# An encoder trunk in split float32: gates, even queries and keys projected by token and turned by DMA

## The chip, the core and the metric

The kernel runs on one core of a Trainium2 chip. A core has five engines with their own instruction streams: TensorE (PE in the profile; PEld is its weight load), VectorE (DVE), ScalarE (ACT), GpSimd (POOL) and SyncE (SP), which here only issues DMAs. The metric is the device time of one execution in microseconds. A run of the profiler gives one execution with a record of each instruction; its span, from the first to the last instruction, is a little shorter than its device time.

## What is computed

A trunk of two pre-RMSNorm residual layers and a final RMSNorm over x of 256 tokens by 2048 features, all float32. The even layer has one input projection for two head groups of eight heads each (head size 128): A is dilated sliding-window attention with an ALiBi penalty, B is 2-D neighbourhood attention with a learned position bias per head. The odd layer has C, windowed grouped-query attention with a sink logit and ALiBi (eight query heads, two key/value heads), and D, dense grouped-query attention with RMS-normalised q and k and axial rotary. Each branch has a gate as wide as its output.

```
def even_layer(y, w_in, w_out, rpb):
    qa, ka, va, ga, qb, kb, vb, gb = _split(y @ w_in, EVEN_SPLITS)
    oa = dilated_attention(heads(qa, A_HEADS), heads(ka, A_HEADS), heads(va, A_HEADS))
    ob = neighbourhood_attention(heads(qb, B_HEADS), heads(kb, B_HEADS), heads(vb, B_HEADS), rpb)
    mix = concatenate([oa * silu(ga), ob * silu(gb)], axis=-1)
    return mix @ w_out
...
    for layer in range(DEPTH):
        y = rms_norm(h, norm_g[layer])
        h = h + (even_layer if layer % 2 == 0 else odd_layer)(y, ...)
    return rms_norm(h, final_g)
```

## The kernel before

**Precision.** Every product of two float32 matrices is made of three products of rounded parts: a value is split into `hi` (rounded, by ScalarE) and `lo` (the rest, by VectorE, L89 to L98), and hi·hi, hi·lo and lo·hi are added up in PSUM.

**Weights.** All projections read their weights in chunks of 128 x 1024 float32 (512 KB). `plan` lists the chunks in the order of use. `Weights` (L54) loads a chunk by a DMA of SP (L65), ScalarE makes `whi` (L69), VectorE `wlo` (L70). `weights()` (L78) makes chunks two ahead of the one in use. There are five buffers for raw chunks and three for `whi` and for `wlo`.

**Two ways to project.** The normalised input, scaled by the norm's weights but not yet by the rows' scale, lies turned in SBUF: feature on the partition, 256 tokens along the row, hi and lo side by side (`xx`). Contraction runs over 16 steps of 128 features.
- `by_feature` (L275) makes a group of 256 columns turned, feature by token. The weights are stationary: for each step and each of two halves of 128 columns one matmul of `whi` over 512 columns (x's hi and lo, which add up in separate halves of the bank) and one of `wlo` over 256 columns (L284, L288). A chunk holds four steps of one group.
- `by_token` (L294) makes the result token by feature. The input is stationary; per step and each of two halves of 128 tokens it takes three matmuls (`mm3`, L102 to L104) as wide as the group: 512, or 256 for C's v. A chunk holds two steps of 512 columns.

Queries, keys and gates were made by feature, in the layout that attention needs; all values, and D's queries and keys, by token. `scaled` (L324) adds the two halves of a feature accumulator and multiplies by the row scale, spread over the partitions by `spread_scale` (L187); `gate` (L342) adds the tanh.

**Attention** works on pairs of heads (`attend`, L423). A pair's two heads give logits on TensorE (`ps_s`), a minimum, an exponential, and a division; the probabilities are turned by DMA: GpSimd splits each 32-bit word into two 16-bit halves (L480), two DMA transposes move them (L87, through `pinned`), GpSimd joins the words again (L491), and the result is split into hi and lo. Then follow the product with the values (`ps_out`), the multiplication with the gate (`mx`, L534) and the split into `mh`, `ml`, the input of the output projection.

**Order.** The program is written out in the order in which TensorE is to work. After each chunk `step()` (L216) lets some of the other work take one step: generators in the queues `evac` (reading accumulators), `post` (D's rotary) and `bg` (attention), each up to its next `yield`. `attention()` steps the first pair that has main work left; a pair that yields True is in its last part and lets the next one go beside it. `need(pr)` (L257) steps without a chunk until the pair that the output projection wants is done. `take` and `room` keep count of buffers. A scheduler may move an instruction ahead on its engine, unless `keep_in_program_order` holds it; `pinned` DMAs are held, a chunk's loads in most places are not.

**The even layer** goes through four units of two pairs (A's four, then B's four), in the order of `even_order` (L571). B's position bias comes from DRAM, where `load_consts` (L144) spreads it over 64 rows; `bias_rpb` (L405) reads it per head in four DMAs of 64 x 4 x 64 and subtracts it from a mask on GpSimd (L420). Then the output projection by token (`project_out`, L649) in quarters of 512 columns, of which the finished ones are turned by the same DMA way into the odd layer's input. **The odd layer** makes D's k and v, D's queries and gates, C's k, v, and then C's q and gate four times, and its output projection, whose order starts with D's pairs.

Of the kernel before, what the change touches and what calls it, by code (L numbers as in the profile page):

```python
# [18 lines left out]
P = 128  # L19
# [17 lines left out]
def encoder(ctx, tc, a, out):  # L37
# [16 lines left out]
    class Weights:  # L54


        def __init__(self, src, hi=None, lo=None, x=None):
            raw = wp.tile([P, 1024], F32, tag="wraw", name="wraw")
# [3 lines left out]
            cols = [slice(i * 1024 // cuts, (i + 1) * 1024 // cuts) for i in range(cuts)]  # L62
            for i, c in enumerate(cols):
                load = nc.sync.dma_start if x is None else pinned
                load(raw[:, c], src[:, c])  # L65
                if x is not None and i == 0:
                    pinned(xraw[x], a["xt"][x].rearrange("p (k t) -> p k t", k=KK))
# [7 lines left out]

    plan, ready = [], []
# [64 lines left out]
    NR = 8 * RPB_R * RPB_C  # L141
    rows = dram.tile([GRID_W, NR], F32, tag="rows", name="rows")

    def load_consts():  # L144
        pinned(rows, a["rpb_b"].rearrange("h r c -> (h r c)").partition_broadcast(GRID_W))
        pinned(maskB, a["mask_b"])
        pinned(cosT, a["cos"])
        pinned(sinT, a["sin"])
        pinned(gq, a["qnorm_d"].partition_broadcast(P))
        pinned(gk, a["knorm_d"].partition_broadcast(P))  # L150
        sink = sm.tile([P, 8], F32, tag="sink", name="sink", bufs=1)
        pinned(sink, a["sinks_c"].partition_broadcast(P))
        nc.gpsimd.tensor_scalar_mul(nsink, sink, -1.0)
# [25 lines left out]
    def row_scale(layer, parts):  # L179

        ss = sm.tile([P, 2], F32, tag="ss", name="ss")
        nc.vector.tensor_reduce(ss, parts, AX.X, ALU.add)
        r = const.tile([P, 2], F32, tag=f"rstd{layer}", name=f"rstd{layer}")
        rsqrt(r, ss, 2, 1.0 / D)
        return r

    def spread_scale(r):  # L187
# [6 lines left out]
        rk = const.tile([P, S], F32, tag="rk", name="rk")  # L194
        rq = const.tile([P, S], F32, tag="rq", name="rq")
        nc.vector.tensor_copy(rk, bc)
        nc.vector.tensor_scalar_mul(rq, rk, -SCALE)
        rhalf = const.tile([P, S], F32, tag="rhalf", name="rhalf")
        nc.vector.tensor_scalar_mul(rhalf, rk, 0.5)
        return rk, rq, rhalf  # L200


    evac, post, bg, done = [], [], [], set()
# [12 lines left out]
    def step():  # L216

        advance(evac)
        advance(post)
        attention()  # L220
# [16 lines left out]
    def drain():  # L237
        while evac or post or bg:
            step()
# [15 lines left out]
    steps = {}  # L255

    def need(pr):  # L257

        while pr not in done:
            assert evac or post or bg  # L260
# [81 lines left out]
    def gate(acc, rhalf):  # L342

        g = scaled(acc, rhalf)
        e = tp.tile([P, 2, S], F32, tag="ge", name="ge", bufs=1)
        nc.scalar.activation(e, g, AF.Tanh)
        s = silu_tile()
        nc.vector.scalar_tensor_tensor(s, e, 1.0, g, ALU.add, ALU.mult)
        return s
# [12 lines left out]
    def normed_rope(tag, q, ss, g, scale, give):  # L362
# [21 lines left out]
        yield  # L384
        yield from room(tag)
# [7 lines left out]
        yield  # L393

# [10 lines left out]
    def bias_rpb(head):  # L405

        raw = tp.tile([P, 2, S], F32, tag="rpb", name="rpb", bufs=1)
        for half in range(2):
            for qt in range(2):
                r = 2 * qt + half  # L410
                at = head * RPB_R * RPB_C + (7 - r) * RPB_C + 15
                src = bass.AP(
                    rows.tensor, rows.offset + at, [[NR - 1, GRID_W], [RPB_C, 4], [1, GRID_W]]
                )
                pinned(
                    raw[half * GRID_W : (half + 1) * GRID_W, qt, :].rearrange("p (r c) -> p r c", r=4), src
                )
        take("bias")
        b = pp.tile([P, 2, S], F32, tag="bias", name="bias", bufs=ROOM["bias"])
        nc.gpsimd.tensor_tensor(b, maskB.unsqueeze(1).to_broadcast([P, 2, S]), raw, op=ALU.subtract)  # L420
        return b

    def attend(idx, q, kv, silu, frees, bias=None, sink=None, shared=False):  # L423

        (qh, ql), (kh, kl), (vh, vl, v0) = q, kv[0], kv[1]
# [76 lines left out]
        def weigh(heads, o):  # L502
            hi, lo = st["p"]
            c = slice(v0 + kvh(heads.start) * P, v0 + kvh(heads.start) * P + P)
            for k in range(2):
                mm3(o[:, heads, :], vh[:, k, c], vl[:, k, c], hi[:, k, heads, :], lo[:, k, heads, :], k == 0, k == 1)

        logits(0)
# [17 lines left out]
        yield  # L526
        o = ps_o.tile([P, 2, S], F32, tag="o", name="ps_out")
# [10 lines left out]
        yield True  # L538

# [31 lines left out]
    def even_order(u):  # L571

        tokens, first = [(None, "v")], [(0, "q"), (0, "k")]
        head = tokens + first if u == 0 else first + tokens
        return head + [(0, "g"), (1, "q"), (1, "k"), (1, "g")]

    for u in range(4):
        for pr, kind in even_order(u):
            if kind == "v":
                plan.extend((a["even_t"][u][j], None if u else j) for j in range(8))  # L580
            else:
                plan.extend((a["even_f"][2 * u + pr]["qkg".index(kind)][j], None) for j in range(4))
    out_plan("even")
    for t, fs in ((0, ()), (1, (10, 11)), (2, (12, 13))):
        plan.extend((a["odd_t"][t][j], None) for j in range(8))
        plan.extend((a["odd_f"][f][j], None) for f in fs for j in range(4))
    plan.extend((a["odd_f"][f][j], None) for f in (0, 1, 2, 6, 3, 7, 4, 8, 5, 9) for j in range(4))
# [14 lines left out]
    def first_scale():  # L602
# [3 lines left out]
        r = row_scale(0, parts0)  # L606
        yield
        yield
        scales[0] = r, spread_scale(r)
        yield  # L610

    def evict_even(p, kind, acc, st):
        r, (rk, rq, rhalf) = scales[0]
        if kind == "v":
            values(st["v"], acc, r)
        elif kind == "q":
            st["q"] = scaled_split("q", acc, rq)
            heads = (2 * (p % 4), 2 * (p % 4) + 1)
            st["bias"] = [bias_table(a["bias_a"][x]) if p < 4 else bias_rpb(x) for x in heads]
        elif kind == "k":  # L620
            st["k"] = scaled_split("k", acc, rk)
        else:
            s = gate(acc, rhalf)
            v = (*st["v"], p % 2 * S)
            bg.append(attend(p, st["q"], (st["k"], v), s, ("q", "k", "silu", "bias", "bias"), st["bias"]))
        yield

    def later_consts():
        load_consts()
        yield  # L630

    for u in range(4):
        st = {}
        if u == 1:
            bg.append(later_consts())
        for pr, kind in even_order(u):
            if kind != "v":
                evac.append(evict_even(2 * u + pr, kind, by_feature(), st))
                continue
            if u:  # L640
# [5 lines left out]
            st["v"] = values_tile()  # L646
            evac.append(evict_even(2 * u, kind, acc, st))
# [74 lines left out]
    r1 = row_scale(1, parts1)  # L722


    evac.append(second_scale())
# [6 lines left out]
    def attend_odd(branch, i, st, s):  # L732
        frees = ["q", "silu"] + ["bias", "bias"] * (branch == 0) + ["k"] * (i == 3)
        kv, heads = (st["k"], (*v, (1 - branch) * S), i // 2), (2 * i, 2 * i + 1)
        bg.append(
            attend(4 * branch + i, st["q", i], kv, s, frees, st.get(("bias", i)), heads if branch == 0 else None, True)
# [7 lines left out]
    def evict_heads(st, which, acc):  # L744

        for i, key in enumerate(which):
            if key is not None:
# [3 lines left out]
                post.append(normed_rope("k" if key == "k" else "q", q, ss, g, scale, give))  # L751
# [208 lines left out]
```

## Time and profile before

| | us |
|---|---|
| median of 3 runs | 817.61 (817.42 to 818.71) |
| profiled execution | 817.19 |
| its span | 815.4 |
| TensorE busy | 805.6 (99%) |
| VectorE busy | 577.7 (71%) |
| ScalarE busy | 447.8 (55%) |
| GpSimd busy | 128.6 (16%) |
| DMA queue of SP, share of 16 engines | 64.3% |

The profile's groups are lines such as "L284 PE MATMUL ps_f<-x,whi ... x1184 | 372.1, 396 | 0.0": source line, engine, operation, what is written from what, shape, count, then busy time in us, mean ns of one, and idle time of the engine before them with what ended it. Matmuls are pipelined, so their durations overlap. A timeline's line has start and length in us, engine, line, operation, and in brackets the idle time before it and what ended it. `ps_f` are accumulators by feature, `ps_t` by token, `wraw`, `whi` and `wlo` a chunk and its two parts, `ph`, `pa`, `pt` the stages of turned probabilities.

### The profile page before, as it was taken

The numbers are of one execution on the slowest core, as the hardware profiler recorded it, in microseconds if no ns is written. First come the engines' busy times: TensorE is split into PE (matmuls) and PEld (weight loads), VectorE is DVE, ScalarE is ACT, GpSimd is POOL, SyncE is SP. The second block draws the span as 40 slices with busy tenths as digits, with TensorE's granted clock in tenths as the row PEclk, the third lists the DMA queues.
The fourth block names the chain that finished last, engine by engine and source line by source line (L and its number), as shares of the span: only waits on it lengthen the run. The fifth ranks groups of instructions, "written<-read, shape, count | busy, mean of one in ns | idle before, by whom it ended". The sixth has DMA issues, their size and how long they took to land.

```text
span 815.4 us, 11762 instructions
## 1 busy us (share of the span) xinstructions
PE 805.6 (99%) x4293; PEld 691.7 (85%) x4293; DVE 577.7 (71%) x855; ACT 447.8 (55%) x712; POOL 128.6 (16%) x100
## 2 busy tenths in 40 slices
PE   9999999999999999999999999999999999999996
PEld 7888888888888888888888888888889888888885
DVE  6677676677857887497656776685987776765863
ACT  7755454555545554455445555657656665664651
POOL 0002020021302240040204300002112223221000
PEclk9999999999999999999999999999999999999998
DMA  9957675565755756566758755566558676767632
GB/s 337 362 200 221 250 228 181 207 206 175 235 176 171 231 164 245 186 186 222 203 184 194 253 198 166 197 203 201 153 179 231 221 213 186 235 196 227 206 133 103
DMA packets 97066, 168.47 MB, mean 207 GB/s; under 512 B 55472, under 2 KB 56368, under 8 KB 96944
## 3 DMA queue, kind: packets, MB, share of 16 engines
q1 hardware_dynamic: 96864, 167.71, 64.3%
q8 instruction: 33, 0.54, 0.3%
q14 instruction: 25, 0.20, 0.1%
q10 hardware_dynamic: 144, 0.02, 0.0%
HBM read 155.64 MB, written 3.05 MB: 195 GB/s over the span
## 4 chain that ended last, share of the span: by engine, by line
PE 98%; DMA 1%; DVE 0%; SPq 0%; ACT 0%; issue 0%; ACTq 0%; DVEq 0%
PE ps_f L284 34%; PE ps_f L288 17%; PE ps_t L103 14%; PE ps_t L104 14%; PE ps_t L102 13%; PE ps_s L104 1%; PE ps_s L103 1%; PE ps_s L102 1%; PE ps_out L103 1%; PE ps_out L102 1%; PE ps_out L104 1%; DMA wraw<-in_even_t 1%; SPq L87 0%; PE ps_tr L389 0%; DVE wlo L70 0%; ACT whi L69 0%
## 5 line engine op out<-in xcount | busy, mean ns | idle before, releaser
L70 DVE TENSOR_TENSOR wlo<-wraw,whi 128x1024 fp32r<-128x1024 f32 (+1 forms) x270 | 346.3, 1283 | 184.6 <-ACT whi L69 183.3
L69 ACT CAST whi<-wraw 128x1024 fp32r<-128x1024 f32 (+1 forms) x270 | 282.2, 1045 | 300.2 <-PE ps_t L104 127.8
L284 PE MATMUL ps_f<-x,whi 128*128 128x512 f32 x1184 | 372.1, 396 | 0.0
L288 PEld LDWEIGHTS ps_f<-x,wlo 128*128 128x128 f32 x1184 | 222.2, 188 | 53.5 <-DVE wlo L70 1.2
L288 PE MATMUL ps_f<-x,wlo 128*128 128x256 f32 x1184 | 233.0, 278 | 0.0
L284 PEld LDWEIGHTS ps_f<-x,whi 128*128 128x128 f32 x1184 | 180.8, 189 | 0.5
L102 PE MATMUL ps_t<-whi,x 128*128 128x512 f32 (+1 forms) x256 | 96.3, 379 | 0.6 <-ACT x L95 0.5
L103 PE MATMUL ps_t<-wlo,x 128*128 128x512 f32 (+1 forms) x256 | 96.1, 377 | 0.1
L104 PE MATMUL ps_t<-whi,x 128*128 128x512 f32 (+1 forms) x256 | 95.9, 377 | 0.0
L480 POOL COPY ph<-pr 128x1024 uint16<-128x1024 uint16 x32 | 39.5, 1235 | 350.8 <-ACT pr L470 182.9
L102 PE MATMUL ps_t<-whi,mh 128*128 128x512 f32 x240 | 93.5, 389 | 0.0
L103 PE MATMUL ps_t<-wlo,mh 128*128 128x512 f32 x240 | 93.5, 389 | 0.0
L104 PE MATMUL ps_t<-whi,ml 128*128 128x512 f32 x240 | 93.4, 389 | 0.0
L491 POOL COPY pt<-pa 128x1024 uint16<-128x1024 uint16 x32 | 51.5, 1608 | 35.8 <-DMA pa<-ph 35.8
L102 PEld LDWEIGHTS ps_t<-whi,x 128*128 128x128 f32 x256 | 48.2, 188 | 9.6 <-ACT x L95 1.3
L104 PEld LDWEIGHTS ps_t<-whi,x 128*128 128x128 f32 x256 | 48.2, 188 | 9.0 <-DVE x L96 0.2
L103 PEld LDWEIGHTS ps_t<-wlo,x 128*128 128x128 f32 x256 | 48.2, 189 | 8.6 <-DVE wlo L70 0.5
L104 PEld LDWEIGHTS ps_t<-whi,ml 128*128 128x128 f32 x240 | 45.1, 188 | 9.3
L102 PEld LDWEIGHTS ps_t<-whi,mh 128*128 128x128 f32 x240 | 45.1, 188 | 9.2
L103 PEld LDWEIGHTS ps_t<-wlo,mh 128*128 128x128 f32 x240 | 45.1, 188 | 9.1
L420 POOL TENSOR_TENSOR bias<-maskB,rpb 128x512 f32<-128x512 f32 x8 | 12.2, 1526 | 137.6 <-DMA rpb<-rows 137.6
L462 ACT ACTIVATE pr<-lg,mn 128x256 f32<-128x256 f32 (+1 forms) x48 | 24.0, 501 | 16.8 <-POOL ph L480 9.2
(133 smaller groups left out, 675.5 us busy)
## 6 DMA issues: line engine op xcount, KB each, us to landing
wraw<-in_even_f SPq DMA_DIRECT2D x96, 512.0 KB, 3.4
wraw<-in_odd_f SPq DMA_DIRECT2D x56, 512.0 KB, 3.6
wraw<-in_w_out_even SPq DMA_DIRECT2D x32, 512.0 KB, 4.1
wraw<-in_w_out_odd SPq DMA_DIRECT2D x32, 512.0 KB, 4.2
wraw<-in_even_t SPq DMA_DIRECT2D x30, 512.0 KB, 4.3
wraw<-in_odd_t SPq DMA_DIRECT2D x24, 512.0 KB, 3.4
xraw<-in_xt SPq DMA_DIRECT2D x8, 256.0 KB, 7.0
h<-in_x SPq DMA_DIRECT2D x4, 512.0 KB, 8.6
```

Of the source, the lines that this page charges most:

```text
L69: nc.scalar.copy(self.hi[:, c], raw[:, c])
L70: nc.vector.tensor_sub(self.lo[:, c], raw[:, c], self.hi[:, c].bitcast(F32))
L102: nc.tensor.matmul(dst, lh, rh, start=first, stop=False, skip_group_check=True)
L103: nc.tensor.matmul(dst, lh, rl, start=False, stop=False, skip_group_check=True)
L104: nc.tensor.matmul(dst, ll, rh, start=False, stop=last, skip_group_check=True)
L284: nc.tensor.matmul(acc[:, f, :], w.hi[:, c], xx[k], start=k == 0, stop=False, skip_group_check=True)
L288: nc.tensor.matmul(acc[:, f, :S], w.lo[:, c], xh[k], start=False, stop=k == KC - 1, skip_group_check=True)
L420: nc.gpsimd.tensor_tensor(b, maskB.unsqueeze(1).to_broadcast([P, 2, S]), raw, op=ALU.subtract)
L462: nc.scalar.activation(p[:, t, :W], lg[:, t, :W], AF.Exp, bias=mn[:, t : t + 1], scale=-1.0, accum_out=den[:, t : t + 1],)
L480: nc.gpsimd.tensor_copy(halves, words)
L491: nc.gpsimd.tensor_copy(words.bitcast(U16).rearrange("p c (q s) -> p s c q", s=2), st[i])
```

## The change

**Projections.** The gates of both layers, the even layer's queries and keys, and C's key become token groups: two groups of 256 columns lie side by side in one accumulator of 512. Their weights in DRAM keep the old layout, so `side_by_side` makes a chunk of two loads, each with 256 columns for two contraction steps. C's value goes beside C's key. C's four queries stay by feature. The even layer's units follow `EVEN`, where g is the two gates of a unit and 0 and 1 are q and k of its pairs.

**Turning.** `evict_turned` scales a group by the rows' scale on ScalarE, and `turned` takes its words apart on ScalarE, moves them by two DMA transposes, joins them on GpSimd, and splits them into hi and lo. `evict_gates` and `gate` do so for gates, with the tanh ahead and the words taken apart on GpSimd. `turn` steps up to two such jobs a step, the second three steps behind the first.

**Attention.** It no longer takes the gate and the values at its start: it waits for the bias tables, for the values ahead of its second product (one pair at a time, `held`), and for the gate ahead of `mx`.

**Small loads.** The constants come one every second step in place of seven at once. A pair's position bias comes in two DMAs of 64 x 2 x 219, one run of 219 values per row and head; GpSimd subtracts windows of it.

```diff
+    def side_by_side(left, right):
+        for j in range(NJ):
+            pieces = []
+            for i, group in enumerate((left, right)):
+                place = lambda raw, i=i: raw.rearrange("p (k c) -> p k c", k=KK)[:, :, i * S : (i + 1) * S]
+                src = group[j // 2].rearrange("p (k c) -> p k c", c=S)
+                pieces.append((place, src[:, j % 2 * KK : (j % 2 + 1) * KK]))
+            plan.append((pieces, None))
...
     def load_consts():
...
+            pinned(dst, src)
+            yield
+            yield
...
         advance(post)
+        advance(prep)
+        advance(once)
+        turn(later)
+        turn(jobs)
         attention()
...
+    def turn(queue):
+        for i, job in enumerate(list(queue)):
+            if i and steps[id(queue[i - 1])] < 3 or i > 1:
+                break
+            steps[id(job)] += 1
+            try:
+                next(job)
+            except StopIteration:
+                steps[id(job)] = 99
+        while queue and steps[id(queue[0])] == 99:
+            steps.pop(id(queue.pop(0)))
...
+    def evict_gates(acc, half, pairs):
+        for i, pr in enumerate(pairs):
+            g = tp.tile([P, 2, S], F32, tag="tmp", name="gf", bufs=4)
+            for t in range(2):
+                nc.scalar.mul(g[:, t, :], acc[t][:, i * S : (i + 1) * S], half[:, t : t + 1])
+            later.append(gate(g, pr))
+            steps[id(later[-1])] = 0
+            yield
+    def gate(g, pr):
+        e = tp.tile([P, 2, S], F32, tag="ge", name="ge")
+        tc.keep_in_program_order(nc.scalar.activation(e, g, AF.Tanh))
+        nc.vector.scalar_tensor_tensor(g, e, 1.0, g, ALU.add, ALU.mult)
+        yield
+        halves = tp.tile([P, 2, 2, S], U16, tag="ge", name="gh")
+        tc.keep_in_program_order(
+            nc.gpsimd.tensor_copy(halves, g.bitcast(U16).rearrange("p t (k s) -> p t s k", s=2))
+        )
+        yield
...
+            pinned(... halves[:, t].rearrange("p s k -> p (s k)"), transpose=True)
+        yield
+        yield
+        yield
+        yield from room("silu")
         s = silu_tile()
-        nc.vector.scalar_tensor_tensor(s, e, 1.0, g, ALU.add, ALU.mult)
-        return s
+        tc.keep_in_program_order(
+            nc.gpsimd.tensor_copy(s.bitcast(U16).rearrange("p c (q s) -> p s c q", s=2), across)
+        )
+        yield
+        gated[pr] = s
+        yield
+    def turned(f, tag, give):
+        words = tp.tile([P, 2, S], F32, tag="tmp2", name="tw")
...
+        pin(nc.scalar.copy(halves, f.bitcast(U16).rearrange("p t (k s) -> p t s k", s=2)))
+        yield
+        for t in range(2):
+            pinned(... halves[:, t].rearrange("p s k -> p (s k)"), transpose=True)
+        yield
+        yield
+        yield
+        pin(nc.gpsimd.tensor_copy(words.bitcast(U16).rearrange("p c (q s) -> p s c q", s=2), across))
+        yield
+        yield from room(tag)
+        dst = pair(tag)
+        split(*dst, words, None, pin)
+        yield
+        give(dst)
+        yield
...
+    def neighbourhoods(first, keep):
+        raw = tp.tile([P, 2, S], F32, tag="rpb", name="rpb", bufs=1)
         for half in range(2):
+            at = first * RPB_R * RPB_C + (5 - half) * RPB_C + 15
+            run = bass.AP(rows.tensor, rows.offset + at, [[NR - 1, GRID_W], [RPB_R * RPB_C, 2], [1, RUN]])
+            pinned(raw[half * GRID_W : (half + 1) * GRID_W, :, :RUN], run)
+            yield
...
         parted(1)
         yield
+        while held or kv[1]() is None:
+            yield
+        held.append(idx)
         o = ps_o.tile([P, 2, S], F32, tag="o", name="ps_out")
...
+        while idx not in gated:
+            yield True
         m = tp.tile([P, 2, S], F32, tag="tmp", name="mx", bufs=4)
-        nc.vector.tensor_mul(m, o, silu)
+        pin(nc.vector.tensor_mul(m, o, gated.pop(idx)))
...
+        held.clear()
...
+    EVEN = ["v 0 g 1", "g 0 v 1", "g 0 v 1", "0 1 v g"]
...
+    for fs in ((0, 1), (2,), (6, 7), (3,), (4,), (8, 9), (5,)):
+        if len(fs) == 2:
+            side_by_side(*(a["odd_f"][f] for f in fs))
```

More of the change, by code (lines that the diff above doesn't have):

```diff
@@ L62, in __init__ @@
             cols = [slice(i * 1024 // cuts, (i + 1) * 1024 // cuts) for i in range(cuts)]
+            if isinstance(src, list):
+                for place, piece in src:
+                    nc.sync.dma_start(place(raw), piece)
             for i, c in enumerate(cols):
                 load = nc.sync.dma_start if x is None else pinned
-                load(raw[:, c], src[:, c])
+                if not isinstance(src, list):
+                    load(raw[:, c], src[:, c])
                 if x is not None and i == 0:
@@ L184, in row_scale @@
         rsqrt(r, ss, 2, 1.0 / D)
-        return r
+        half, minus = [const.tile([P, 2], F32, tag=f"{x}{layer}", name=f"{x}{layer}") for x in ("half", "minus")]
+        nc.vector.tensor_scalar_mul(half, r, 0.5)
+        nc.vector.tensor_scalar_mul(minus, r, -SCALE)
+        return r, half, minus
     def spread_scale(r):
@@ L193, in spread_scale @@
             nc.tensor.transpose(bc[:, tt * P : (tt + 1) * P], t, ident)
-        rk = const.tile([P, S], F32, tag="rk", name="rk")
         rq = const.tile([P, S], F32, tag="rq", name="rq")
[L196 to L203, printed above, removed]
+        nc.vector.tensor_scalar_mul(rq, bc, -SCALE)
+        return rq
+    evac, post, later, prep, once, bg, held, done, gated = [], [], [], [], [], [], [], set(), {}
     live = {"q": 0, "k": 0, "silu": 0, "bias": 0}
@@ L360, in heads_by_token, with normed_rope @@
         return q, ss
-    def normed_rope(tag, q, ss, g, scale, give):
+    def normed_rope(tag, q, ss, g, scale, give, begin):
         rr = sm.tile([P, 4], F32, tag="drr", name="drr")
@@ L403, in bias_table, with tables, attend @@
         return b
-    def bias_rpb(head):
+    def tables(src, keep):
+        for s in src:
+            yield from room("bias")
+            keep.append(bias_table(s))
+            yield
+    def neighbourhoods(first, keep):
         raw = tp.tile([P, 2, S], F32, tag="rpb", name="rpb", bufs=1)
         for half in range(2):
-            for qt in range(2):
[L410 to L425, printed above, removed]
+            at = first * RPB_R * RPB_C + (5 - half) * RPB_C + 15
+            run = bass.AP(rows.tensor, rows.offset + at, [[NR - 1, GRID_W], [RPB_R * RPB_C, 2], [1, RUN]])
+            pinned(raw[half * GRID_W : (half + 1) * GRID_W, :, :RUN], run)
+            yield
+        yield
+        for i in range(2):
+            yield from room("bias")
+            take("bias")
+            b = pp.tile([P, 2, S], F32, tag="bias", name="bias", bufs=ROOM["bias"])
+            for qt in range(2):
+                w = raw[:, i, 2 * (1 - qt) * RPB_C :]
+                window = bass.AP(w.tensor, w.offset, [list(w.ap[0]), [RPB_C, 4], [1, GRID_W]])
+                pin(nc.gpsimd.tensor_tensor(
+                    b[:, qt, :].rearrange("p (r c) -> p r c", r=4), maskB.rearrange("p (r c) -> p r c", r=4), window,
+                    op=ALU.subtract,
+                ))
+            keep.append(b)
+            yield
+    def attend(idx, q, kv, frees, bias=None, sink=None, shared=False):
+        (qh, ql), (kh, kl) = q, kv[0]
         kvh = lambda i: kv[2] if shared else i
@@ L506, in weigh @@
                 mm3(o[:, heads, :], vh[:, k, c], vl[:, k, c], hi[:, k, heads, :], lo[:, k, heads, :], k == 0, k == 1)
+        while bias is not None and len(bias) < 2:
+            yield
         logits(0)
@@ L721, in encoder @@
     project_out("even", next_input)
-    r1 = row_scale(1, parts1)
+    r1, half1, _ = row_scale(1, parts1)
+    done.clear()
     evac.append(second_scale())
```

168 lines of the change are left out of this document (91 added, 77 removed).

## The prediction

> **What bounds the kernel now.** I read the page from the top (engine totals, the chain that ended last), then TensorE's timeline at three places, then the groups by shape, and last the DMA queue and the weights' way from load to use.
>
> ```profile
> span 815.4 us, 11762 instructions
> PE 805.6 (99%) x4293; PEld 691.7 (85%) x4293; DVE 577.7 (71%) x855; ACT 447.8 (55%) x712; POOL 128.6 (16%) x100
> PE 98%; DMA 1%; DVE 0%; SPq 0%; ACT 0%; issue 0%; ACTq 0%; DVEq 0%
> ```
>
> The chain is TensorE for 98% of the span: outside the opening and the closing microseconds nobody keeps it waiting, so the time is a sum of matmuls. Their durations overlap, so a matmul's price is the distance from start to start. Three stretches give it:
>
> ```profile
> 24.10 0.39 PE L102 MATMUL ps_t<-whi,x 128*128 128x512 f32 x1
> ...
> 26.82 0.39 PE L102 MATMUL ps_t<-whi,x 128*128 128x512 f32 x1
> ...
> 99.85 0.63 PE L284 MATMUL ps_f<-x,whi 128*128 128x512 f32 x2
> ...
> 103.33 0.62 PE L284 MATMUL ps_f<-x,whi 128*128 128x512 f32 x2
> ...
> 104.03 0.28 PE L102 MATMUL ps_s<-kh,qh 128*128 128x256 f32 x1
> ...
> 104.75 0.40 PE L284 MATMUL ps_f<-x,whi 128*128 128x512 f32 x1
> ```
>
> By token, one weight chunk is 12 matmuls of 512 columns: 24.10 to 26.82 is 2.72 us, 0.2267 each. By feature, 99.85 to 103.33 holds five of the 128-row steps of the contraction, each two matmuls of 512 and two of 256 columns: 0.696 a step. Six lone matmuls of 256 columns take 0.72 us, 0.120 each. From 0.120 and 0.2267 a matmul costs about 0.107 us for every 256 columns and 0.013 for itself; by feature that makes 6 x 0.107 + 4 x 0.013 = 0.694, as measured. So both ways stream the same columns, and the token way has three matmuls where the feature way has four.
>
> **The matmuls.** The shapes' counts:
>
> ```profile
> L284 PE MATMUL ps_f<-x,whi 128*128 128x512 f32 x1184 | 372.1, 396 | 0.0
> L288 PE MATMUL ps_f<-x,wlo 128*128 128x256 f32 x1184 | 233.0, 278 | 0.0
> L102 PE MATMUL ps_t<-whi,x 128*128 128x256 f32 x32 | 9.1, 283 | 0.0
> ```
>
> 1184 / 32 = 37 feature groups of 256 columns: 24 even ones (q, k, gate of eight head pairs), 13 odd ones (C's k, four q, four gates, D's four gates). The change leaves C's four q by feature and makes the other 33 token groups, two side by side in 512 columns. C's v, by token 256 wide (three lines of 32), joins C's k. Removed: 33 x 16 x 0.696 = 367.5 us and 96 x 0.120 = 11.5. Added: 34 groups, 17 accumulators x 16 x 6 = 1632 matmuls x 0.2267 = 370.0. Net -9.0 us, all of it on the path. Two small transposes of the even layer's row scale go as well (-0.1).
>
> **Evictions.** Per shape:
>
> ```profile
> L327 ACT COPY qf<-ps_f 128x512 f32<-128x512 f32 x37 | 21.4, 577 | 0.0
> L328 DVE TENSOR_TENSOR qf<-ps_f,qf 128x512 f32<-128x512 f32 x37 | 25.3, 682 | 0.0
> L329 DVE TENSOR_TENSOR qf<-qf,rhalf 128x512 f32<-128x512 f32 x16 | 11.1, 692 | 0.5
> L355 ACT ACTIVATE rq<-ps_t,rstd 128x256 f32<-128x256 f32 x10 | 4.4, 469 | 0.0
> L69 ACT CAST whi<-wraw 128x1024 fp32r<-128x1024 f32 x266 | 279.7, 1052 | 297.8 <-PE ps_t L104 127.8 <-PE ps_f L284 108.1 <-issue 35.1
> L480 POOL COPY ph<-pr 128x1024 uint16<-128x1024 uint16 x32 | 39.5, 1235 | 350.8 <-ACT pr L470 182.9 <-DVE pr L472 159.1 <-ACT whi L69 8.8
> L491 POOL COPY pt<-pa 128x1024 uint16<-128x1024 uint16 x32 | 51.5, 1608 | 35.8 <-DMA pa<-ph 35.8
> L420 POOL TENSOR_TENSOR bias<-maskB,rpb 128x512 f32<-128x512 f32 x8 | 12.2, 1526 | 137.6 <-DMA rpb<-rows 137.6
> ```
>
> VectorE loses an add and a multiply per group: 33 x (0.682 + 0.692) = 45.3 us, 577.7 to about 532. ScalarE loses 33 x 0.577 = 19.0, gains two scaled copies a group (66 x 0.469 = 31.0) and 17 word splits of heads; no row has that copy, so I bound it by the cast of as many elements, 1.05, and GpSimd's word copies, 1.61, and take 1.05 as the same engine's: 17.9. It ends near 478. GpSimd gains 33 rejoining copies (x 1.608 = 53.1) and 16 gate splits (x 1.235 = 19.8), 128.6 to 202; the bias subtraction keeps its elements. No engine comes near the 806 us that TensorE keeps, so on average all this is hidden behind matmuls. VectorE's relief is not all its own, for it slows beside a GpSimd copy:
>
> ```profile
> 300.52 1.36 POOL L491 COPY pt<-pa 128x1024 uint16<-128x1024 uint16 x1
> 301.03 1.86 DVE L70 TENSOR_TENSOR wlo<-wraw,whi 128x1024 fp32r<-128x1024 f32 x1 [1.36 <-ACT whi L69]
> 307.62 1.21 DVE L70 TENSOR_TENSOR wlo<-wraw,whi 128x1024 fp32r<-128x1024 f32 x1
> ```
>
> 1.86 beside a copy, 1.21 alone: 49 more copies cost VectorE between nothing and 49 x 0.65 = 32 us; at the upper end it stands at 564, still below the 577.7 of now.
>
> **The DMA queue.** SP issues in order:
>
> ```profile
> 300.96 2.54 SPq L87 DMA_TRANSPOSE pa<-ph  x2
> 298.95 1.90 SPq L87 DMA_DIRECT2D rpb<-rows  x3
> 98.40 0.90 SPq L87 DMA_DIRECT2D bias<-in_bias_a  x2
> 293.64 0.33 SPq L65 DMA_DIRECT2D wraw<-in_even_t  x1
> ```
>
> A transpose holds SP 1.27 us, and 66 come on top (two for each of 33 groups): 84 us. 136 of the weight chunks become two loads of 1 KB pieces; a piece load costs between 0.45 (bias table) and 0.63 (rpb rows), I take the bias table, whose tile has the piece's shape (128 x 2 x 256), so +0.57 a chunk, 78 us. The position bias gives back: 32 loads of 0.63 become 8, -15. Over eight chunks (8 x 2.72 = 21.8 us) SP then has 8 x 0.90 for weights, 4 x 1.27 for the groups' transposes and 2 x 1.27 for the probabilities': 14.8 us, 17.7 at the higher piece price. It keeps up. The reordering of small loads (one every second step in place of seven at once) touches no wait of TensorE and I cost it at nothing; it is covered by what covers the weights:
>
> ```profile
> wraw<-in_even_f SPq DMA_DIRECT2D x96, 512.0 KB, 3.4
> 305.52 1.05 ACT L69 CAST whi<-wraw 128x1024 fp32r<-128x1024 f32 x1
> 311.08 0.40 PE L102 MATMUL ps_t<-whi,x 128*128 128x512 f32 x1
> 311.32 0.40 PE L103 MATMUL ps_t<-wlo,x 128*128 128x512 f32 x1
> ```
>
> The chunk issued at 293.64 is cast at 305.52, 11.9 us later, of which the transfer needs some 3.4: 8.5 to spare. Its low half ends at 307.62 + 1.21 = 308.83 and is wanted at 311.32: 2.5 more.
>
> **Order and new waits.** I counted the yields, one step per chunk. A q/k group turns its scaled copy over about eight steps (split, transposes, three idle steps, rejoin, hi/lo), and a gate likewise, two at a time. Attention therefore starts some eight steps after its k, and its last multiply waits for the gate (the new loop ahead of `mx`). Behind that multiply on VectorE are weight subtractions, but it is issued only in a step after the gate was rejoined, so they gain no wait. The places where TensorE would have nothing but attention to do are the output projections: counted from the last even group, pair 6 is done in step 6 and wanted in step 12, pair 7 in step 9 and wanted in step 14. In the odd layer pair 3 is done in step 12 and wanted in step 14, as before. No loop of `need` turns without weights: 0 us. If the cover is gone by a step, it costs that step's 2.7 us once.
>
> **The opening** is where loads are late already:
>
> ```profile
> 26.45 1.05 ACT L69 CAST whi<-wraw 128x1024 fp32r<-128x1024 f32 x1 [2.25 <-DMA wraw<-in_even_f]
> ...
> 28.18 0.61 PE L284 MATMUL ps_f<-x,whi 128*128 128x512 f32 x2
> 28.82 0.39 PE L288 MATMUL ps_f<-x,wlo 128*128 128x256 f32 x1
> ```
>
> This is the first chunk after the v group. ScalarE waited 2.25 us for it, and TensorE started its low half 0.64 after two matmuls that take 0.47: it is late by 0.17. This chunk becomes two loads. Its transfer could come 0.2 us earlier in effect or 2.3 later (the wait doubled); I take +0.5, nearer to the small end, since the bytes are the same.
>
> Sum: 815.4 - 9.1 + 0.5 = 806.8 span. The profiled execution took 817.19, so 1.8 lies around the span: 808.6. The median shown, 817.61, is 0.4 above the profiled one, of which I add a part: **808.8**.
>
> **The rivals.**
> A, a part is given back (811 to 816). Steps bunch: a rejoining copy, a subtraction that it slows by 0.65, a split and an attention reduction in one chunk use up the 2.5 us that the weights' low half has. If each of 16 attention passes costs 0.3 us, that is 4.8: 813.6. For it: the 1.86 row. Against: VectorE has less work than before and the trace shows no such stall now.
>
> B, SP makes it slower. Place: the steps in which a gate's or head's transposes meet the probabilities'. Six transposes (7.6 us) and two chunks of pieces (1.8) are 9.4 us in two steps of 5.4, and each pinned transpose also waits for its word split, so a weight load queued behind them goes late by 4.0 plus these waits. Up to 8.5 + 2.5 = 11 us lateness is covered; beyond that each microsecond is TensorE's. With 16 such meetings it takes 0.57 us at each to eat the 9.1, and above that the change loses; at 1 us each, 808.8 + 16 = 825. For it: transposes keep their place in the order. Against: the 11 us, and loads that are not pinned can be put ahead of them.
>
> C, no saving. The 0.013 us would not belong to the matmul, and only columns would count. The columns are equal, so 817.2, plus the opening's 0.5: 817.7. Against it stands that the new groups have the very form of the 0.2267 row. The Trainium skill ("TensorE: Matmul & The Clock Gate", section "Back-to-back issue gap") is near this: a warm matmul starts N / 2.4 + 2.5 ns after the last, so an estimate from that page is 0.216 us at 512 and 0.109 at 256, both below the rows here, and the change would then save about 1.5 us.
>
> **How the numbers follow.** Forecast (807 to 811): 0.68. A: 0.13. C: 0.05. B: 0.14. The range leaves out B and C, 0.19, and reaches from 806 (opening free, sum a little better) to 816.5. A measurement of this kernel tells about 0.2%, 1.6 us, from no change: faster is below 816.0 (forecast and A, 0.81), within is C and the edge of B (0.06), slower 0.13.
>
> **What would show it.** Right: L284 with 128 matmuls, the token form with 1632 more at 0.2267 from start to start, TensorE at 98% or more of the chain with an idle time of some 10 us in all, VectorE 530 to 565, ScalarE near 478, GpSimd near 200. Wrong: weight loads or casts late on TensorE's rows, with SP's transposes ahead of them (B); subtractions as releasers of TensorE (A); a token matmul further than 0.23 from the next with nobody awaited (C).

## The result and the profile after

The changed kernel takes 809.71 us (median of 4 runs, 809.23 to 810.55) against 817.51; the ratio is 0.9903, 95% interval 0.9885 to 0.992. The forecast was 808.8. The profiled execution took 810.08, its span is 808.3: 7.1 less than before, where the sum had 8.6. Of the executions in the experiments below one, with the doubled transposes, took 1350 us at a mean granted clock of 0.56, where its fellows had 0.99; why is open, and the ratio there is formed without it.

The totals and the chain of the changed kernel's page:

```profile
span 808.3 us, 10993 instructions
PE 796.2 (99%) x3715; PEld 665.0 (82%) x3715; DVE 550.2 (68%) x786; ACT 469.4 (58%) x762; POOL 213.1 (26%) x157
PE 93%; DVE 2%; DMA 2%; POOL 1%; issue 1%; ACT 0%; SPq 0%; ACTq 0%; POOLq 0%; DVEq 0%
```

TensorE has 578 matmuls fewer (4293 to 3715) and is still busy for 99% of a shorter span. VectorE lost 27.5 us, ScalarE and GpSimd gained 21.6 and 84.5. The chain gives TensorE five points less than before. That is not five points of waiting: the chain is read back from a single wait at 580 us and leaves TensorE's row at about 543 us for other engines, on which TensorE was in truth at work all the while.

TensorE's groups by shape, and a stretch of its timeline with the new groups at work:

```profile
L118 PE MATMUL ps_t<-whi,x 128*128 128x512 f32 x768 | 299.7, 391 | 1.5 <-ACT x L111 1.5
L324 PE MATMUL ps_f<-x,whi 128*128 128x512 f32 x128 | 40.2, 395 | 0.0
L328 PE MATMUL ps_f<-x,wlo 128*128 128x256 f32 x128 | 25.1, 278 | 0.0
```

```profile
200.03 0.39 PE L119 MATMUL ps_t<-wlo,x 128*128 128x512 f32 x1
...
202.75 0.39 PE L119 MATMUL ps_t<-wlo,x 128*128 128x512 f32 x1
```

Twelve matmuls of a turned group take 2.72 us, 0.2267 each, the same as the v group of the kernel before. There are 768 per line where there were 224, in three lines: the 1632 of the sum. To see where the 7.1 us lie, I divide both profiled executions at the same two matmuls. One is the first of the last contraction step of the opening v group, which comes first in both kernels and which the change leaves as it was (the 91st matmul of the projections); the prediction shows it for the kernel before, at 26.82. The other is the last matmul of all. In the changed kernel they are

```profile
27.72 0.39 PE L118 MATMUL ps_t<-whi,x 128*128 128x512 f32 x1
...
799.24 0.28 PE L120 MATMUL ps_e<-x,ml 128*128 128x256 f32 x1
```

and the last matmul of the kernel before is

```profile
807.27 0.28 PE L104 MATMUL ps_e<-x,ml 128*128 128x256 f32 x1
```

So the opening is 0.9 us longer than before (27.72 against 26.82), the stretch between the two matmuls 8.9 shorter (771.52 against 780.45), and the closing part 0.9 longer (9.0 against 8.1). All that the change does to TensorE's work lies in this middle stretch; its length is given for the experiments too, since the opening moves from one execution to the next.

The one new wait of the middle stretch is in D's part of the odd layer. TensorE, VectorE and GpSimd of the changed kernel there:

```profile
579.76 0.39 PE L118 MATMUL ps_t<-whi,x 128*128 128x512 f32 x1
580.66 0.50 PE L119 MATMUL ps_t<-wlo,x 128*128 128x512 f32 x1 [0.52 <-DVE wlo L75]
```

```profile
572.96 1.01 DVE L192 SCALAR_TENSOR_TENSOR rs_z<-rs_t,rs_y 128x4 f32<-128x4 f32 x1
574.00 1.23 DVE L189 TENSOR_TENSOR rs_t<-rs_z 128x4 f32<-128x4 f32 x1
575.26 0.16 DVE L190 SCALAR_TENSOR_TENSOR rs_t<-rs_t,rs_x 128x4 f32<-128x4 f32 x1
575.37 1.22 DVE L75 TENSOR_TENSOR wlo<-wraw,whi 128x1024 fp32r<-128x1024 f32 x1
...
577.29 2.19 DVE L473 SCALAR_TENSOR_TENSOR rq<-rq,drr,gq 128x128 f32<-128x128 f32 x4
579.40 1.21 DVE L75 TENSOR_TENSOR wlo<-wraw,whi 128x1024 fp32r<-128x1024 f32 x1
```

```profile
572.37 1.58 POOL L601 COPY ph<-pr 128x1024 uint16<-128x1024 uint16 x1 [5.36 <-ACT pr L591]
573.90 1.36 POOL L612 COPY pt<-pa 128x1024 uint16<-128x1024 uint16 x1
577.88 1.51 POOL L612 COPY pt<-pa 128x1024 uint16<-128x1024 uint16 x1 [2.62 <-DMA pa<-ph]
```

The second matmul should start 0.23 after the first and starts 0.90 after it: the chunk's low half was ready at 579.40 + 1.21. Ahead of that subtraction VectorE had D's reciprocal root and four multiplies (2.19). Two of the tiny steps of the root, 0.16 each as a rule, took 1.01 and 1.23: they end, within 0.03, where two GpSimd copies end (573.95 and 575.26).

### The profile page after: what moved, and what is told of

Read it like the earlier page. It is cut to its first block, busy times and chain, and to the rows that moved or that the text cites. A ratio compares the mean times of both kernels' runs of the same rounds, so it can differ in the third digit from the quotient of the medians.

```text
span 808.3 us, 10993 instructions
## 1 busy us (share of the span) xinstructions
PE 796.2 (99%) x3715; PEld 665.0 (82%) x3715; DVE 550.2 (68%) x786; ACT 469.4 (58%) x762; POOL 213.1 (26%) x157
## 4 chain that ended last, share of the span: by engine, by line
PE 93%; DVE 2%; DMA 2%; POOL 1%; issue 1%; ACT 0%; SPq 0%; ACTq 0%; POOLq 0%; DVEq 0%
PE ps_t L119 27%; PE ps_t L120 27%; PE ps_t L118 27%; PE ps_f L324 4%; PE ps_f L328 2%; DVE wlo L75 1%; PE ps_s L120 1%; PE ps_s L119 1%; DMA wraw<-in_even_t 1%; PE ps_s L118 1%; PE ps_out L120 1%; PE ps_out L119 1%; PE ps_out L118 1%; DMA wraw<-in_odd_f 1%; SPq L103 0%
## 5 line engine op out<-in xcount | busy, mean ns | idle before, releaser
L75 DVE TENSOR_TENSOR wlo<-wraw,whi 128x1024 fp32r<-128x1024 f32 (+1 forms) x270 | 353.5, 1309 | 206.2 <-ACT whi L74 197.8
L118 PE MATMUL ps_t<-whi,x 128*128 128x512 f32 x768 | 299.7, 391 | 1.5 <-ACT x L111 1.5
L119 PE MATMUL ps_t<-wlo,x 128*128 128x512 f32 x768 | 299.1, 390 | 0.6 <-DVE wlo L75 0.5
L120 PE MATMUL ps_t<-whi,x 128*128 128x512 f32 x768 | 298.5, 389 | 0.0
L118 PEld LDWEIGHTS ps_t<-whi,x 128*128 128x128 f32 x768 | 144.2, 188 | 31.2 <-ACT x L111 2.6
L120 PEld LDWEIGHTS ps_t<-whi,x 128*128 128x128 f32 x768 | 144.2, 188 | 30.6 <-DVE x L112 0.2
L119 PEld LDWEIGHTS ps_t<-wlo,x 128*128 128x128 f32 x768 | 144.3, 188 | 29.7 <-DVE wlo L75 1.5
L400 POOL COPY gh<-gf 128x1024 uint16<-128x1024 uint16 x16 | 19.8, 1239 | 141.0 <-DVE gf L396 125.5
L447 POOL COPY tw<-tf 128x1024 uint16<-128x1024 uint16 x17 | 26.1, 1538 | 114.5 <-DMA tf<-tw 110.6
L324 PE MATMUL ps_f<-x,whi 128*128 128x512 f32 x128 | 40.2, 395 | 0.0
L621 DVE TENSOR_TENSOR ptl<-pt,pth 128x512 fp32r<-128x512 f32 x32 | 28.9, 908 | 3.8 <-ACT pth L620 3.8
L415 POOL COPY silu<-gf 128x1024 uint16<-128x1024 uint16 x16 | 28.7, 1797 | 4.3 <-DMA gf<-gh 4.3
```

What stands on the lines that cost most here:

```text
L75: nc.vector.tensor_sub(self.lo[:, c], raw[:, c], self.hi[:, c].bitcast(F32))
L118: nc.tensor.matmul(dst, lh, rh, start=first, stop=False, skip_group_check=True)
L119: nc.tensor.matmul(dst, lh, rl, start=False, stop=False, skip_group_check=True)
L120: nc.tensor.matmul(dst, ll, rh, start=False, stop=last, skip_group_check=True)
L324: nc.tensor.matmul(acc[:, f, :], w.hi[:, c], xx[k], start=k == 0, stop=False, skip_group_check=True)
L415: nc.gpsimd.tensor_copy(s.bitcast(U16).rearrange("p c (q s) -> p s c q", s=2), across)
```

## The experiments

All times are medians. The runs were timed in three groups, each with the kernel before beside it: the first four below (818.01), then the busier queue, the small loads put back, the words on GpSimd and the gates alone (818.28), then the other four (817.5). The changed kernel itself was timed again in the first group alone, so ratios to "before" are the safer comparison across groups.

### The changed kernel again

> The changed kernel once more, as the measure for the others of this call. Every theory expects 809.7 us within 0.8. It also shows which of the small losses of its trace come back: the 0.7 us stall at 580 us (order of the program, so in every execution) and the 0.9 us longer stores at the end and the 0.5 us longer first chunks (expected to move from run to run).

809.46 us (ratio 0.9897, 0.9884 to 0.9911). Its trace has the stall at 580 us again, of the same length, so that one belongs to the program. Its middle stretch is again 771.5 us. The closing part is again 9.0 long, against my expectation that it would vary; the opening varied, 27.3 in place of 27.7.

### The matmul's own price

```diff
-        nc.tensor.matmul(dst, ll, rh, start=False, stop=last, skip_group_check=True)
+        for q in [slice(0, 256), slice(256, 512)] if cut else [slice(None)]:
+            nc.tensor.matmul(dst[:, q], ll, rh[:, q], start=False, stop=last, skip_group_check=True)
```

`cut` is set in the 17 accumulators of the new token groups.

> In the 17 accumulators that the change made token groups, the third matmul of each three is cut into two of 256 columns: 544 matmuls and weight loads more, the same columns and the same sums. Theory M (a matmul costs 0.013 us for itself, and the change gains by having fewer): +544 x 0.0133 = +7.2, 816.9 us, nearly the time before. Rival O (the gain comes from work that VectorE or the queues lost, and columns alone count on TensorE): no change, 809.7.

817.0 us, 7.5 more than the changed kernel in the same group; ratio to before 0.9988 (0.9979 to 0.9997). Theory M named 816.9, rival O 809.7. TensorE's timeline in this kernel, through a group of the even layer that is cut:

```profile
200.19 0.39 PE L119 MATMUL ps_t<-wlo,x 128*128 128x512 f32 x1
200.42 0.40 PE L121 MATMUL ps_t<-whi,x 128*128 128x256 f32 x2
200.66 0.40 PE L118 MATMUL ps_t<-whi,x 128*128 128x512 f32 x1
...
203.68 0.40 PE L119 MATMUL ps_t<-wlo,x 128*128 128x512 f32 x1
```

From 200.19 to 203.68 there are five times three products, in 20 matmuls: 0.698 for each three products with the cut, where the uncut three take 3 x 0.2267 = 0.680, and a step by feature took 0.696. With TensorE's work the same to the column and everything that the change moved left in place, putting back about the number of matmuls that it removed (544 for 578) puts back nearly all of the time. The middle stretch says so more sharply: 779.7 us, 8.2 more than in the changed kernel, or 0.0150 for each matmul put back. So the gain is the number of matmuls, each of which comes with a weight load of its own; the experiment does not part the two.

### Whole loads

The chunks of two groups are laid out in DRAM beforehand; `side_by_side` becomes

```diff
+        n = sides.pop(0)
+        plan.extend((a["side"][n][j], None) for j in range(NJ))
```

> The 136 chunks of two groups are laid side by side in DRAM beforehand and come in one load of 4 KB rows each, in place of two loads of 1 KB pieces. Theory M: the loads are hidden, 809.7 within 0.5, at best 0.3 less in the opening. Rival S (SP's queue, with 136 more issues and smaller packets, holds weights back here and there): 1 to 2 us less, 808.0, and the stall at 580 us gone.

809.36 us, 0.1 less than the changed kernel, ratio 0.9896 (0.9882 to 0.9909): no difference that can be told. The stall at 580 us stays. The 136 more issues cost nothing as the kernel stands.

### Transposes twice, and twice with whole loads

```diff
+        twice = tp.tile([P, 4, P], U16, tag="twice", name="twice", bufs=1)
         for t in range(2):
-            pinned(
-                across[:, :, :, t * P : (t + 1) * P].rearrange("p s c q -> p (s c) q"),
-                halves[:, t].rearrange("p s k -> p (s k)"), transpose=True,
-            )
+            for dst in (across[:, :, :, t * P : (t + 1) * P].rearrange("p s c q -> p (s c) q"), twice):
+                pinned(dst, halves[:, t].rearrange("p s k -> p (s k)"), transpose=True)
```

> Each of the 66 new DMA transposes of heads and gates is issued twice, the second time to a tile that nobody reads: 66 x 1.27 = 84 us more of SP's issuing, and as many more packets. Theory M: loads have about 11 us to spare, so 809.7 within 1. Rival S (SP near its limit): some of the 16 meetings with the probabilities' transposes exceed the 11 us, and it takes 815 or more.

837.48 us, 28 more (ratio 1.0239, 1.0226 to 1.0253). Theory M failed here, but the experiment was not clean: there is one spare tile, so each second transpose waits for the landing of the one before, with weight loads behind it in the queue. Later I ran the same with whole loads:

> The doubled transposes once more (837.5 us), now with the two-piece chunks laid out beforehand and loaded whole: 136 issues and 75 us less of SP's time, and fewer DMAs in flight. The doubled transposes still have one spare tile and wait for it. Theory Q (weights came late because the queue was full: issuing time, and a DMA that waits for the landing of the eighth before it): most of the 28 us go, 810 to 817. Theory W (the waits on the spare tile alone held the queue): 30 us stay, 832 or more.

832.57 us (ratio 1.0185, 1.0171 to 1.0199). Theory Q (810 to 817) failed, and theory W's bound (832 or more) was met. Giving back 136 issues gives back 5 of the 28 us. So it is not SP's issuing time in sum that makes the loss. Nor is it the sum of SP's own waits for the spare tile: these are 9.9 us with loads in pieces and 23.6 with whole loads, in the faster of the two. Whether the rest is the wait for the spare tile, as theory W has it, or the bunching of transposes ahead of loads, these two runs cannot tell apart, for they change both.

### A busier queue

```diff
             pinned(... halves[:, t].rearrange("p s k -> p (s k)"), transpose=True)
+            for _ in range(4):
+                idler = dram.tile([P, 1], F32, tag=f"idler{len(idlers)}", name="idler")
+                idlers.append(idler)
+                pinned(idler, warm)
```

> Behind each of the 132 halves' transposes of heads and gates stand four stores of 4 bytes a row to DRAM, each to a place of its own, so nobody waits for them and they wait for nothing: 264 issues of about 0.43 us, 114 us more of SP's time, more than the doubled transposes took (84), and hardly any bytes. Theory W (the doubled transposes cost 28 us because each waited for the landing of the one before into its one spare tile, with the weight loads queued behind): at most 2 us more than the changed kernel, 809.5 to 811.5. Rival S (SP's issuing time alone is near its limit): 825 or more.

1875.8 us, which neither theory had: both took it that nobody waits for these stores. (The expectation's count of 132 transposes is wrong: the 264 stores stand behind 66, four each.) The longest waits of SP in this kernel (us in total, times, longest):

```profile
SPq L103 <- DMA idler<-warm: 465.1, 93, 18.0
SPq L66 <- DMA idler<-warm: 225.3, 47, 10.1
SPq L70 <- DMA idler<-warm: 72.1, 14, 10.3
```

SP itself waits for the stores to land, 762 us in all, in front of transposes and of weight loads (L66, L70). The program's DMAs on this queue take eight semaphores in turn (in the changed kernel's trace 76 issues on each of eight), and each DMA first waits until the one before it on its semaphore has landed. So no more than eight are in flight (eight is the most that the changed kernel's trace has between issue and landing), and a slow one holds the eighth behind it whatever that is. The experiment says nothing of issuing time; it showed the queue's depth.

### The small loads put back

```diff
             pinned(dst, src)
-            yield
-            yield
         yield
```

and in `neighbourhoods` the four loads a head of the kernel before, with one subtraction for each head.

> Undoes the small loads alone: all seven constants are issued at once, and the position bias comes in four loads a head as before (32 in place of 8, 15 us more of SP). Theory M: this is hidden, 809.5 within 0.6. Rival S (the queue is near its limit, and the change needed this relief): 2 us more or worse, with TensorE waiting near the burst and in the units of B.

814.57 us, 5.1 more than the changed kernel (ratio to before 0.9957, 0.9945 to 0.9969); the middle stretch is 5.3 longer, 776.8 us. Theory M failed: the queue did need this relief. SP and a piece of the chain that ended last, then ScalarE and TensorE of this kernel, where the constants come:

```profile
92.97 0.62 SPq L103 DMA_DIRECT2D rows<-in_rpb_b  x1
93.63 0.57 SPq L103 DMA_DIRECT2D maskB<-in_mask_b  x1
...
96.39 0.43 SPq L103 DMA_DIRECT2D sink<-in_sinks_c  x1
96.92 2.17 SPq L66 DMA_DIRECT2D wraw<-in_even_f  x2
```

```profile
92.97 5.73 DMA rows<-in_rpb_b
98.70 0.02 issue
98.72 7.42 DMA wraw<-in_even_f
```

```profile
106.23 1.04 ACT L74 CAST whi<-wraw 128x1024 fp32r<-128x1024 f32 x1 [6.38 <-DMA wraw<-in_even_f]
```

```profile
105.60 0.39 PE L120 MATMUL ps_t<-whi,x 128*128 128x512 f32 x1
107.33 0.49 PE L118 MATMUL ps_t<-whi,x 128*128 128x512 f32 x1 [1.34 <-ACT whi L74]
...
109.38 0.63 PE L118 MATMUL ps_t<-whi,x 128*128 128x512 f32 x1
109.81 0.63 PE L119 MATMUL ps_t<-wlo,x 128*128 128x512 f32 x1
```

Read them downwards: the spread of the position bias (DRAM to DRAM, issued at 92.97) is on the chain of this kernel until it lands at 98.70. The second piece of the weight load at 96.92 is the eighth DMA behind it, has its semaphore and cannot go before that. ScalarE stands 6.38 us for that chunk, and TensorE waits twice. From 108.6 to 112.1 the granted clock is then 0.54, and the matmuls come 0.43 apart: the stall costs its own 2.5 us and 1.6 us more of half speed. A second, smaller stall (0.8 us) is at 349 us, in a unit of B. To see why the same burst cost nothing before, I put it back with whole loads:

> The small loads as before (all constants at once, the bias in four loads a head: 5.1 us more than the changed kernel), now with whole loads of the weights. Theory Q (the pieces have eaten the cover that the burst had in the kernel before): at least 3 of the 5.1 us come back, 809.5 to 811.5. Theory K (the burst itself is too long for any queue, since its first DMA, DRAM to DRAM, holds what comes behind): 813 or more.

811.02 us (ratio 0.9917, 0.9904 to 0.9929). That is 3.6 us less than with pieces, or 2.8 when each is set against the kernel before of its own group; in the middle stretch (772.6) 4.2 of the 5.3 come back. Theory Q has it better than theory K, whose 813 was not reached; one stall of 1.1 us is left at that place. The chunk in two pieces takes two of the eight places in flight and twice the issues, so the same burst reaches further. And the small loads by themselves, in the kernel before (`load_consts` of the change, stepped from `post`; `bias_rpb` with the two loads a pair):

> The kernel before with the change's small loads alone: constants one every second step, position bias as one run a row, nothing else. Every theory that puts the gain in the matmuls: no change, 817.8 within 0.6, since TensorE waits for none of these loads there. A theory in which the small loads gain by themselves: 2 us less or more.

818.47 us, ratio 1.0008 (0.9999 to 1.0017), the middle stretch 780.2 against 780.5: nothing. This part of the change gains nothing; it keeps the rest from losing 5 us.

### Words of heads on GpSimd

```diff
-        pin(nc.scalar.copy(halves, f.bitcast(U16).rearrange("p t (k s) -> p t s k", s=2)))
+        pin(nc.gpsimd.tensor_copy(halves, f.bitcast(U16).rearrange("p t (k s) -> p t s k", s=2)))
```

> The words of the 17 turned head groups are taken apart by GpSimd in place of ScalarE: 17 x 1.24 = 21 us more on GpSimd, 18 less on ScalarE, and up to 17 x 0.65 = 11 us more on VectorE beside them. Theory M: all of it hidden, 809.5 within 0.6. Rival A (lateness of GpSimd and VectorE reaches TensorE): 1 to 4 us more, in the steps where a head's turn meets a gate's.

810.5 us, 0.4 above theory M's bound; ratio 0.9906 (0.9893 to 0.9919) beside 0.9897 (0.9884 to 0.9911) of the changed kernel in the first group. The intervals overlap, and the traces' waits differ only in the opening, ahead of any turned head; the middle stretch is 771.4 us, as without it: no effect that can be told. Which engine takes the words apart did not matter.

### The gates alone

The even layer's queries and keys go back to feature groups:

```diff
-                side_by_side(*(a["even_f"][2 * u + int(kind)][i] for i in range(2)))
+                plan.extend((a["even_f"][2 * u + int(kind)][i][j], None) for i in range(2) for j in range(4))
...
+                evac.append(evict_even(u, kind + "q", by_feature()))
+                evac.append(evict_even(u, kind + "k", by_feature()))
```

with the row scale spread over the partitions for them, as before.

> One part alone: the even layer's queries and keys (16 groups) go back to feature groups, with 64 KB... of weight loads whole again for them; gates and C's key stay by token. Theory M: 16 x 16 steps x 0.0163 = 4.2 us more on TensorE, 0.2 for two transposes: 813.8 within 0.7. A theory in which gates bring the gain and the heads' turns are paid back by their transposes (32 fewer here): 809.5 or less.

815.41 us (ratio 0.9966, 0.9954 to 0.9979), 5.9 more than the changed kernel and 0.9 beyond theory M's bound. The middle stretch is 776.8 us, 5.2 longer. 256 matmuls more, at the 0.0163 of the expectation, are 4.2 of it; the other 1.0 is waiting: logits now follow their key too closely, as the weight loads of TensorE show in this kernel:

```profile
PEld ps_s L119 <- DVE kl L109: 1.1, 4, 0.3
```

The 0.7 us between this and the medians' 5.9 are not assigned. Heads thus bring 4.2 us of the gain by their matmuls; that the turn by DMA gives nothing of that back is read from the changed kernel's trace, where no wait of TensorE leads to it.

### One more step in the rotary

```diff
         rsqrt(rr, ss, 4, 1.0 / HD)
+        yield
         for i in range(4):
```

with whole loads.

> Whole loads, and one more yield in D's rotary between the reciprocal root and the four multiplies, so that the weights' subtraction of a later chunk can go between them. Theory A (the stall of 0.7 us at 580 us and the 0.2 behind it come from VectorE's burst there): that stall is gone, 0.9 us less than with whole loads alone: 808.4. If the stall is a matter of loads: 809.4 and the stall stays.

809.32 us, ratio 0.9895 (0.988 to 0.991), the same as whole loads alone, where 808.4 was expected. In its trace the stall is gone: VectorE now has the subtraction between the multiplies,

```profile
577.67 0.35 DVE L471 SCALAR_TENSOR_TENSOR rq<-rq,drr,gq 128x128 f32<-128x128 f32 x1
577.95 1.22 DVE L75 TENSOR_TENSOR wlo<-wraw,whi 128x1024 fp32r<-128x1024 f32 x1
579.08 0.87 DVE L471 SCALAR_TENSOR_TENSOR rq<-rq,drr,gq 128x128 f32<-128x128 f32 x3
```

and ready at 579.17, in place of 580.61. So the stall was VectorE's burst, as theory A had it. The median does not show the 0.9 us: 0.35 of it came up as a wait at 599 us, and the opening of the profiled execution was longer (27.7 in place of 26.6). From the end of the v group to the last matmul this trace is 0.8 shorter than the one of whole loads (769.2 against 770.1). None of these versions beats the changed kernel by a measurable amount.

## Why the prediction held, step by step

**The matmuls** (-9.0, with two small transposes -9.1): right. The middle stretch lost 8.9 us with the new stall of 0.7 in it, and the cause is shown by the cut third: 544 matmuls cost 7.5 us by the medians and 8.2 in the middle stretch, 0.0138 or 0.0150 each. The sum's 0.013 was a little small for its own rows, which give 0.016 for each matmul saved (0.696 for four against 0.680 for three); the sum went by the rows. The rival without a saving (C) is out: its premise, that only columns count, is what that experiment contradicts. The saving of about 1.5 us that stands beside C, at 2.5 ns a matmul, did not come out either: 8.9 us for 578 matmuls are 15 ns each.

**Evictions** (hidden): right. VectorE was forecast between 532 and 564 and has 550.2, ScalarE 478 and has 469.4, GpSimd 202 and has 213.1. The rows of the changed kernel:

```profile
L437 ACT COPY tw<-tf 128x1024 uint16<-128x1024 uint16 x17 | 17.7, 1044 | 0.0
L447 POOL COPY tw<-tf 128x1024 uint16<-128x1024 uint16 x17 | 26.1, 1538 | 114.5 <-DMA tf<-tw 110.6
L415 POOL COPY silu<-gf 128x1024 uint16<-128x1024 uint16 x16 | 28.7, 1797 | 4.3 <-DMA gf<-gh 4.3
```

The word split took 1.04 on ScalarE, the lower of my two bounds, which I had chosen. Where it runs made no measurable difference.

**The DMA queue** (keeps up): right for the kernel as changed (whole loads change nothing), but the cover that I gave as the reason was too large. I called the reordering of small loads free because "it is covered by what covers the weights", 11 us of lead in one quoted load. That load was issued ahead of a run of pinned DMAs. The next loads come behind that run, and the first of them brings the chunk of the next cast:

```profile
303.60 0.53 SPq L65 DMA_DIRECT2D wraw<-in_even_t  x1
```

```profile
308.31 1.05 ACT L69 CAST whi<-wraw 128x1024 fp32r<-128x1024 f32 x1 [1.22 <-PE ps_f L284]
```

From issue to cast that is 4.7 us, of which the transfer needs some 3.4: in the kernel before, 1.3 us were to spare and not 8.5. In the changed kernel, with the burst back, the cover is used up at 105 us, and the kernel loses 5.1. What I left out is the depth of the queue, eight DMAs in flight, of which a chunk in two pieces takes two. Rival B had the right place for a loss, a pinned run of DMAs ahead of weight loads, but not the whole measure: I reckoned issuing time, while at this stall the deciding quantity is the landing of the eighth DMA before. The small loads were a condition of the gain and not a side matter.

**Order** (0): right. In the changed kernel TensorE waits neither at the even output projection nor at the odd one, and the new wait of `mx` for the gate shows nowhere.

**The opening** (+0.5): 0.9 in these two traces, but wrong in its place. The first chunk after the v group came in time: the 0.17 us of lateness there is gone in the changed kernel, though it showed up once with whole loads (0.43). What moves is the first 13 us, and from run to run: the 91st matmul starts at 26.6 us with whole loads and at 28.4 in the kernel before with the small loads alone. As a size for the change, 0.5 is neither borne out nor refuted.

**What the sum lacked**: rival A came true once and not sixteen times: 0.9 us at and behind 580 us, from D's rotary and GpSimd's copies on VectorE, shown by the added step. And 0.9 us in the closing part: from the last matmul to the end of the span it is 9.0 us, and 8.1 in the kernel before, with the same instructions on the same engines up to the last stores. The last store is issued 4.8 after that matmul in both and lands 8.0 after it in place of 7.2. The closing part was 9.0 to 9.3 in the other variants of the changed kernel but 8.1 in the one with the cut third; why the stores land later stays open.

**How near it came.** The middle stretch missed the sum by 0.2, the opening by 0.4, the closing part by 0.9: together the 1.5 us between 806.8 and 808.3. The median came within 0.9 of the forecast because it lies 1.4 above the profiled span, where I had put 2.0; that part is luck.

**The signs named ahead** were there (128 by feature, 1632 more by token at 0.2267), except the chain's 98%, which one stall brought to 93% without the time that this seems to say, and the idle time of TensorE, 12.1 us where some 10 were named.

## What to carry to other kernels

Where TensorE is the whole chain, count matmuls and not only columns: a form that streams the same columns in three instructions in place of four gains the fixed price of one, here 14 to 16 ns each, and an experiment that cuts matmuls without changing columns tells it. What such a change moves to DMA must be reckoned in DMAs in flight and their landing too, not in bytes or issuing time alone; spread slow or bunched small loads out on the queue that feeds the weights, and judge the cover by the load that stands behind such a bunch. And undo the parts of a change that seem to gain nothing one at a time: one of them may hold the others up.

## What the runs showed of the hardware

- Matmuls with their weight loads started 0.2267 us apart at 512 columns and 0.120 at 256. Read as one price for 256 columns and one for the matmul itself, that is 0.107 and 0.0133; cutting one matmul of 512 columns into two cost 0.0138 by the medians and 0.0150 by the middle stretch.
- A wait of TensorE of 1.5 us and another of 1.0, one matmul apart, were followed by 3.5 us at a granted clock of 0.54 (matmuls 0.43 apart in place of 0.23), so a stall of 2.5 us cost about 4. The Trainium skill ("TensorE: Matmul & The Clock Gate", section "Why this matters for your kernels") tells to leave no idle gap of more than about 3 us; here two shorter ones were followed by half speed. A single wait of 1.1 us at the same place (small loads with whole loads) was not: matmuls went on 0.23 apart.
- Steps of VectorE on 4 elements a row, 0.16 us each, took 1.01 and 1.23 beside GpSimd's copies, and ended within 0.03 of the copies' ends. A long subtraction beside a copy took 1.86 in place of 1.21.
- Stores of 4 bytes a row to DRAM (264 of them, 128 rows each) lengthened the kernel by 1066 us; SP's own waits for their landing are 762 us of it.
